# Merging two 256-column matmuls into one of 512 columns in four feed-forward networks, and making the norm's factor on all partitions

## The chip, the cores and the metric

The kernel runs on one core of a Trainium2 chip. Times are device microseconds of one execution, from its start to its end. TensorE (PE in the profile) multiplies matrices, VectorE (DVE), ScalarE (ACT) and GpSimd (POOL) do elementwise work, SyncE (SP) issues the loads of weights.

## What is computed

Two blocks of a network follow one another on a sequence of 256 tokens with 1024 features, in float32. The first block has two layers, each with an FFN, an attention mixer and another FFN; the second block has one mixer and one FFN with a convolution. The part that the change touches is the FFN of the first block, which occurs four times:

```python
def rms_norm(x, g):
    xf = x.astype(jnp.float32)
    y = xf * lax.rsqrt(jnp.mean(xf * xf, axis=-1, keepdims=True) + EPS)
    return (y * g.astype(jnp.float32)).astype(x.dtype)

def swiglu(h, w_gate, w_up, w_down):
    return (jax.nn.silu(h @ w_gate) * (h @ w_up)) @ w_down

    h = rms_norm(x, ffn1_norm[layer])
    x = x + 0.5 * swiglu(h, ffn1_w_gate[layer], ffn1_w_up[layer], ffn1_w_down[layer])
```

The hidden width is 2816, so that gate and up are 1024 x 2816 each and down is 2816 x 1024.

## The kernel before

Features lie on the partitions and the 256 tokens (T) in the columns: `x` is eight tiles of 128 x 256. To keep float32 accuracy with the faster matmul type fp32r, every operand is split in two: a high part (the value rounded to fp32r) and a low part (the rest). A product of two operands then takes three matmuls: high by high, the weights' high part by the activations' low part, the weights' low part by the activations' high part. `mm3` (L301 to L305) issues these three, each with a 128 x 128 block of weights as the stationary operand and 256 columns of activations as the moving one; the program issues a weight load (PEld in the profile) for every matmul.

**Weights.** They arrive as blocks of 128 x 1024 (512 KB), eight stationary blocks each, over five raw buffers (L262). `prep` (L277) makes the high part `wh` on ScalarE (L288) and the low part `wl` mostly on VectorE (L290), in five buffers each; a `wh` can only be written when the matmuls on the block five earlier have ended. A block lasts for eight calls of `mm3`.

**One FFN** (`ffn`, L451). The norm of a row of tokens is one factor per token, so it is applied after the matmul. `norm_tile` (L380) splits `x` times the gain into `xh` (ScalarE, L383) and `xl` (VectorE, L384) and adds up the squares in `acc` on GpSimd (L387, L390). For each of the 22 tiles of 128 hidden features there is a gate product `pg` and an up product `pu`, of eight `mm3` each (`proj_t`, L307). They go round six PSUM banks (`six_ps`): the seventh product of an FFN needs the bank of the first. VectorE multiplies `pg` by the factor `rb` (L464), ScalarE takes the Silu (L466), VectorE multiplies by `pu` (L468), and the result is split into `hh` (ScalarE, L469) and `hl` (VectorE, L470). Then come the eight tiles of the down product, 22 `mm3` each; VectorE scales each (L484), adds it to `x` (L486), and the next norm's split follows. All in all an FFN has 352 + 176 = 528 calls of `mm3`.

**The norm's factor** (`norm_end`, called after the first two products). Two fp32 matmuls with the tokens as stationary columns and a single column of ones (L401) give the sums of squares as a column; ScalarE and GpSimd make the reciprocal root of 128 x 2 numbers (L410 to L416); ScalarE spreads it on a diagonal (L424), and a matmul of ones with that (L430) and a copy (L432) give `rb`, the factor on all partitions.

**Order.** The program is recorded as written above and a scheduler with a model of its own then sets the order on each engine. Every engine executes its own list in order, so an instruction that waits holds up all behind it on that engine. After the last FFN of the first block, `trans_tile` takes the place of `norm_tile`, and the next products (`def_proj`, 258 columns) start on its outputs `dh` and `dl` (L934, L935).

Of the kernel before, what the change touches and what calls it, by code (L numbers as in the profile page):

```python
# [210 lines left out]
class K:  # L211
# [121 lines left out]

    def xh(self, k):
        return self.xht[k // 4][:, (k % 4) * T:(k % 4 + 1) * T]

    def xl(self, k):
        return self.xlt[k // 4][:, (k % 4) * T:(k % 4 + 1) * T]
# [37 lines left out]
    def norm_begin(self):  # L376
        self.xht = [self.slot(f"xh{i}", F32R) for i in range(2)]
        self.xlt = [self.slot(f"xl{i}", F32R) for i in range(2)]
# [65 lines left out]

    def ln_exp_tables(self):

        with self.tc.issue_after(self.last_act.ins):
            self.nc.scalar.preload_act_table_set("natural_log_exp_and_others")


    def ffn(self, next_gain):  # L451
        nc = self.nc
        hh = [self.slot(f"hh{i}", F32R) for i in range(6)]
        hl = [self.slot(f"hl{i}", F32R) for i in range(6)]
        h = lambda t, k: t[k // 4][:, (k % 4) * T:(k % 4 + 1) * T]
        for i in range(KF):
            pg = self.six_ps()[:, :T]
            self.proj_t(pg)
            pu = self.six_ps()[:, :T]
            self.proj_t(pu)  # L460
            if i == 0:
                self.norm_end()
            s = self.tmp("s", T)
            nc.vector.tensor_tensor(out=s, in0=pg, in1=self.rb, op=ALU.mult)  # L464
            sg = self.tmp("sg", T)
            self.last_act = nc.scalar.activation(sg, s, AF.Silu)  # L466
            hp = self.tmp("hp", T)
            nc.vector.tensor_tensor(out=hp, in0=pu, in1=sg, op=ALU.mult)  # L468
            nc.scalar.activation(h(hh, i), hp, AF.Copy)  # L469
            nc.vector.tensor_tensor(out=h(hl, i), in0=hp, in1=h(hh, i).bitcast(F32), op=ALU.subtract)  # L470
# [4 lines left out]
        for j in range(KD):  # L475
            ps = self.mm_ps()[:, :T]
            for k in range(KF):
# [831 lines left out]
    def ffn2(self, first):  # L1309
        nc = self.nc  # L1310
        hh = [self.slot(f"hh{i}", F32R) for i in range(6)]
        hl = [self.slot(f"hl{i}", F32R) for i in range(6)]
        h = lambda t, k: t[k // 4][:, (k % 4) * T:(k % 4 + 1) * T]
        x2 = [self.slot(f"x2n{i}") for i in range(2)]
        for i in range(KF):
# [19 lines left out]
            nc.scalar.activation(h(hh, i), hp, AF.Copy)  # L1335
            nc.vector.tensor_tensor(out=h(hl, i), in0=hp, in1=h(hh, i).bitcast(F32), op=ALU.subtract)
# [13 lines left out]
        for gi, (c0, cw) in enumerate(((0, 512), (512, 256), (768, 256))):  # L1350
            ps = [self.mm_ps()[:, :cw] for _ in range(2)]
            held = []
            for k in range(KF):
# [8 lines left out]
                for tt in range(1 if late else 2):  # L1362
                    self.down(ps[tt], h, hh, hl, k, tt, w)
            for tt in range(2):
                if tt:
                    for k, w in held:
                        self.down(ps[1], h, hh, hl, k, 1, w)
# [28 lines left out]
    def down(self, ps, h, hh, hl, k, tt, w):  # L1396
        s = slice(tt * P, (tt + 1) * P)
        self.mm3n(ps, h(hh, k)[:, s], h(hl, k)[:, s], *w, k == 0, k == KF - 1)
# [84 lines left out]
```

## Time and profile before

| | |
|---|---|
| median of 3 runs | 1401.05 us (1400.18 to 1401.47) |
| the profiled execution | 1400.71 us |
| its span, first to last instruction | 1398.9 us |
| TensorE busy | 1346.7 us, 10278 matmuls |
| VectorE busy | 944.0 us |
| ScalarE busy | 751.7 us |

Some 1.8 us of the profiled execution lie around the span. A row of a timeline gives the start and the length of an instruction in microseconds, the engine, the line, the output and inputs by the program's names, the shape, and in brackets the engine's idle time before it and what ended that. Matmuls are pipelined: a record is longer than the time that the matmul occupies the array, so the pace is read from the distance of two starts, not from the length. "x2" on an fp32 matmul means that it is recorded as two passes. Rows by group give how many instructions there were, their busy time and the mean of one in ns.

### The profile page before, as it was taken

What the parts mean: (1) busy time and instruction counts of PE and PEld (TensorE: products, weight loads), DVE (VectorE), ACT (ScalarE), POOL (GpSimd) and SP (SyncE); (2) the same over time, 40 slices, a digit from 0 to 9 for tenths busy, and PEclk for the clock granted to TensorE, in tenths of its full rate; (3) what the DMA queues carried; (4) which work ended last, traced back from release to release, by engine and by line L of the source; (5) the groups of instructions that cost most, each with busy time, mean ns of one, the idle gap of its engine ahead of it and who ended that gap; (6) DMA issues with size and microseconds to landing.
All of it is one profiled execution on the core that took longest, in us unless ns stands there. A gap on an engine that the chain in (4) does not pass through costs nothing.

```text
span 1398.9 us, 26087 instructions
## 1 busy us (share of the span) xinstructions
PE 1346.7 (96%) x10278; PEld 1283.9 (92%) x10278; DVE 944.0 (67%) x1621; ACT 751.7 (54%) x1300; POOL 304.9 (22%) x371
## 2 busy tenths in 40 slices
PE   6999999699999999999999999999989998989997
PEld 6999998489999999999989899999977888889987
DVE  6666556867666656665549866666778768787754
ACT  5544445655444445444458755445566555666642
POOL 4000045442000110000234340001254114541101
PEclk9999999899999999999999999999999998899999
DMA  7555665125555555655565346655646314265561
GB/s 251 181 182 182 184 192 180 31 76 182 182 182 186 180 186 183 184 181 181 184 228 192 121 151 182 182 184 186 185 154 194 106 47 151 76 183 179 185 213 56
DMA packets 64266, 231.70 MB, mean 166 GB/s; under 512 B 7240, under 2 KB 7376, under 8 KB 64144
## 3 DMA queue, kind: packets, MB, share of 16 engines
q1 hardware_dynamic: 61632, 221.41, 50.6%
q0 software_dynamic: 2512, 8.64, 1.8%
q8 instruction: 80, 1.31, 0.4%
q14 instruction: 42, 0.34, 0.1%
HBM read 228.96 MB, written 1.06 MB: 164 GB/s over the span
## 4 chain that ended last, share of the span: by engine, by line
PE 88%; DVE 6%; POOL 2%; ACT 2%; issue 1%; DMA 0%; DVEq 0%; SPq 0%; ACTq 0%
PE mm L303 19%; PE mm L304 18%; PE mm L305 18%; PE sc L304 5%; PE sc L305 5%; PE sc L303 5%; PE mm L331 4%; PE mm L329 4%; PE mm L330 4%; DVE wl L290 2%; PE mm L557 2%; POOL acc L390 1%; PE aux L548 1%; POOL sq L387 1%; ACT wh L288 1%
## 5 line engine op out<-in xcount | busy, mean ns | idle before, releaser
L288 ACT ACTIVATE wh<-raw 128x1024 fp32r<-128x1024 f32 (+1 forms) x425 | 443.3, 1045 | 512.7 <-issue 255.8
L290 DVE TENSOR_TENSOR wl<-raw,wh 128x1024 fp32r<-128x1024 f32 (+1 forms) x406 | 511.3, 1262 | 272.0 <-ACT wh L288 270.4
L303 PE MATMUL mm<-xh,wh 128*128 128x256 f32 x1328 | 380.0, 287 | 11.2 <-ACT xh L383 5.8
L304 PE MATMUL mm<-xl,wh 128*128 128x256 f32 x1328 | 380.6, 287 | 5.7 <-DVE xl L384 5.5
L305 PE MATMUL mm<-xh,wl 128*128 128x256 f32 x1328 | 378.6, 285 | 0.3 <-DVE wl L290 0.3
L303 PEld LDWEIGHTS mm<-xh,wh 128*128 128x128 f32 x1328 | 257.2, 194 | 14.1 <-issue 6.2
L304 PEld LDWEIGHTS mm<-xl,wh 128*128 128x128 f32 x1328 | 257.2, 194 | 9.2 <-DVE xl L384 7.6
L305 PEld LDWEIGHTS mm<-xh,wl 128*128 128x128 f32 x1328 | 257.5, 194 | 1.4 <-issue 0.7
L303 PE MATMUL mm<-hh,wh 128*128 128x256 f32 x704 | 199.2, 283 | 0.0
L304 PE MATMUL mm<-hl,wh 128*128 128x256 f32 x704 | 199.2, 283 | 0.0
L305 PE MATMUL mm<-hh,wl 128*128 128x256 f32 x704 | 199.2, 283 | 0.0
L303 PE MATMUL sc<-xh,wh 128*128 128x256 f32 x560 | 158.9, 284 | 1.9 <-DVE wgb L955 1.9
L304 PE MATMUL sc<-xl,wh 128*128 128x256 f32 x560 | 159.5, 285 | 0.0
L305 PE MATMUL sc<-xh,wl 128*128 128x256 f32 x560 | 159.2, 284 | 0.0
L387 POOL TENSOR_TENSOR sq<-xt 128x256 f32<-128x256 f32 x48 | 36.5, 763 | 507.3 <-DVE xt L486 472.1
L303 PEld LDWEIGHTS mm<-hh,wh 128*128 128x128 f32 x704 | 135.2, 192 | 0.0
L304 PEld LDWEIGHTS mm<-hl,wh 128*128 128x128 f32 x704 | 135.2, 192 | 0.0
L305 PEld LDWEIGHTS mm<-hh,wl 128*128 128x128 f32 x704 | 135.2, 192 | 0.0
L303 PEld LDWEIGHTS sc<-xh,wh 128*128 128x128 f32 x560 | 107.9, 193 | 2.1 <-ACT xt L911 2.1
L305 PEld LDWEIGHTS sc<-xh,wl 128*128 128x128 f32 x560 | 108.0, 193 | 0.1
L304 PEld LDWEIGHTS sc<-xl,wh 128*128 128x128 f32 x560 | 108.0, 193 | 0.1
L331 PE MATMUL mm<-wh,xl 128*128 128x512 f32 x144 | 56.0, 396 | 2.6 <-DVE xl L913 2.6
(348 smaller groups left out, 2242.7 us busy)
## 6 DMA issues: line engine op xcount, KB each, us to landing
raw<-wst SPq DMA_DIRECT2D x417, 512.0 KB, 3.6
m1b<-m1bias POOLq DMA_DIRECT2D x8, 512.0 KB, 5.2
xt<-xT SPq DMA_DIRECT2D x4, 256.0 KB, 4.9
patf<-m2pat POOLq DMA_DIRECT2D x2, 512.0 KB, 6.9
kb<-scr POOLq DMA_DIRECT2D x2, 512.0 KB, 4.7
out<-x2n SPq DMA_DIRECT2D x4, 256.0 KB, 2.0
raw<-wst SPq DMA_DIRECT2D x2, 256.0 KB, 3.7
m0tab<-m0tab POOLq DMA_DIRECT2D x1, 512.0 KB, 3.9
```

Source lines behind the costliest of these rows:

```text
L288: self.nc.scalar.activation(wh[:, c], r[:, c], AF.Copy)
L290: e.tensor_tensor(out=wl[:, c], in0=r[:, c], in1=wh[:, c].bitcast(F32), op=ALU.subtract)
L303: mm(ps, wh, xh, start=first, stop=False)
L304: mm(ps, wh, xl, start=False, stop=False)
L305: mm(ps, wl, xh, start=False, stop=last)
L329: mm(ps, xh, wh, start=first, stop=False)
L330: mm(ps, xh, wl, start=False, stop=False)
L331: mm(ps, xl, wh, start=False, stop=last)
L387: nc.gpsimd.tensor_tensor(out=sq, in0=self.x(j), in1=self.x(j), op=ALU.mult)
L390: self.last_acc = nc.gpsimd.tensor_tensor(out=acc, in0=sq, in1=self.acc, op=ALU.add)
L548: nc.tensor.transpose(ps[:, kt, qt * P:(qt + 1) * P], p[:, qt, kt * P:(kt + 1) * P], self.ident)
L557: self.nc.tensor.matmul(po[half * 64:half * 64 + 64, :T], v[kt], pT[:, kt], start=kt == 0, stop=kt == 1)
```

## The change

`mm3` is replaced by `mm2` in the gate, up and down products of the four FFNs. The high and low parts of the activations now lie side by side, so that one matmul of the weights' high part takes both as 512 moving columns; its output is a whole PSUM bank whose left half holds the products with the high part and whose right half those with the low part. The weights' low part is still multiplied by the high activations alone, with 256 columns, into the left half. `fold` adds the two halves: ScalarE copies the right half out of PSUM, VectorE adds the left half to it. This is one more instruction on each of the two engines for every product. `norm_bcast` replaces `norm_end` in these four FFNs: one fp32 matmul of a 128 x 128 block of ones with `acc` gives the sum on all partitions, and ScalarE and VectorE make the factor there on 128 x 256. The other stages keep `mm3` and `norm_end`; in the last FFN only the layout of the hidden tiles changes.

```diff
+    def mm2(self, ps, wh, wl, x2, first, last):
+
+        mm = self.nc.tensor.matmul
+        if first:
+            mm(ps, wh, x2, start=True, stop=False)
+        mm(ps[:, :T], wl, x2[:, :T], start=False, stop=False, skip_group_check=True)
+        if not first:
+            mm(ps, wh, x2, start=False, stop=last)
...
-            self.mm3(ps, wh[:, s], wl[:, s], self.xh(k), self.xl(k), k == 0, k == KD - 1)
+            if ps.shape[1] == 2 * T:
+                self.mm2(ps, wh[:, s], wl[:, s], self.x2(k), k == 0, k == KD - 1)
+            else:
+                self.mm3(ps, wh[:, s], wl[:, s], self.xh(k), self.xl(k), k == 0, k == KD - 1)
...
+    def both(t, k):
+        return t[k // 2][:, (k % 2) * 2 * T:(k % 2 + 1) * 2 * T]
...
+    def norm_bcast(self):
+
+        nc = self.nc
+        ps = self.aux_ps()[:, :T]
+        nc.tensor.matmul(ps, self.ones, self.acc, start=True, stop=True)
+        u, y, t = [self.tmp(f"nb{i}", T) for i in range(3)]
+        nc.scalar.activation(u, ps, AF.Identity, scale=1.0 / D, bias=self.eps[:, 0:1])
+        nc.scalar.activation(y, u, AF.Ln)
+        nc.scalar.activation(y, y, AF.Exp, scale=-0.5)
+        nc.vector.scalar_tensor_tensor(out=t, in0=y, scalar=-0.5, in1=y, op0=ALU.mult, op1=ALU.mult)
+        nc.vector.tensor_tensor(out=t, in0=t, in1=u, op=ALU.mult)
+        self.rb = self.tmp("rb", T)
+        nc.vector.scalar_tensor_tensor(out=self.rb, in0=t, scalar=1.5, in1=y, op0=ALU.add, op1=ALU.mult)
...
         for i in range(KF):
-            pg = self.six_ps()[:, :T]
+            pg = self.six_ps()
             self.proj_t(pg)
-            pu = self.six_ps()[:, :T]
+            pu = self.six_ps()
             self.proj_t(pu)
             if i == 0:
-                self.norm_end()
+                self.norm_bcast()
             s = self.tmp("s", T)
-            nc.vector.tensor_tensor(out=s, in0=pg, in1=self.rb, op=ALU.mult)
+            self.fold(s, pg)
+            nc.vector.tensor_tensor(out=s, in0=s, in1=self.rb, op=ALU.mult)
             sg = self.tmp("sg", T)
             self.last_act = nc.scalar.activation(sg, s, AF.Silu)
             hp = self.tmp("hp", T)
-            nc.vector.tensor_tensor(out=hp, in0=pu, in1=sg, op=ALU.mult)
...
+            self.fold(hp, pu)
+            nc.vector.tensor_tensor(out=hp, in0=hp, in1=sg, op=ALU.mult)
...
-                self.mm3(ps, wh[:, s], wl[:, s], h(hh, k), h(hl, k), k == 0, k == KF - 1)
+                self.mm2(ps, wh[:, s], wl[:, s], self.both(h2, k), k == 0, k == KF - 1)
             t = self.tmp("t", T)
-            nc.vector.scalar_tensor_tensor(out=t, in0=ps, scalar=0.5, in1=self.rb,
+            self.fold(t, ps)
+            nc.vector.scalar_tensor_tensor(out=t, in0=t, scalar=0.5, in1=self.rb,
                                            op0=ALU.mult, op1=ALU.mult)
...
+    def fold(self, out, ps):
+
+        self.nc.scalar.activation(out, ps[:, T:], AF.Copy)
+        self.nc.vector.tensor_tensor(out=out, in0=ps[:, :T], in1=out, op=ALU.add)
```

The scheduler sets the order anew. On TensorE, the start of the second product of the first FFN (into the bank `mm_245` before, `mm_236` now), which stands for all products of the four FFNs. Before:

```order
L303 MATMUL mm_245<-xh0_108,wh_191 128x256
L304 MATMUL mm_245<-xl0_110,wh_191 128x256
L305 MATMUL mm_245<-xh0_108,wl_192 128x256
L303 MATMUL mm_245<-xh0_108,wh_191 128x256
L304 MATMUL mm_245<-xl0_110,wh_191 128x256
```

Now:

```order
L305 MATMUL mm_236<-xs0_108,wh_190 128x512
L306 MATMUL mm_236<-xs0_108,wl_191 128x256 x2
L308 MATMUL mm_236<-xs0_108,wh_190 128x512
L306 MATMUL mm_236<-xs1_109,wl_191 128x256
L308 MATMUL mm_236<-xs1_109,wh_190 128x512
```

Three matmuls of 256 columns have become one of 512 and one of 256, and the two lengths alternate; nothing else comes between them.

On ScalarE, from the norm's first step in the second FFN (`ffn20`) to the first two banks that are read. Before, `mm_3720` and `mm_3751` are the first two products, read by VectorE alone:

```order
L410 ACTIVATE nw1_3787<-aux_3782,eps_104 128x2
L288 ACTIVATE wh_3812<-raw_3575 128x1024
L411 ACTIVATE nw0_3786<-nw1_3787 128x2
L412 ACTIVATE nw0_3786<-nw0_3786 128x2
L424 ACTIVATE dg_3796<-ident_95,rc_3785 128x128 x2
L288 ACTIVATE wh_3843<-raw_3621 128x1024
L288 ACTIVATE wh_3882<-raw_3667 128x1024
L432 ACTIVATE rb_3801<-aux_3799 128x256
L466 ACT_TABLE_LOAD
L466 ACTIVATE sg_3805<-s_3803 128x256
```

Now, with `mm_3285` and `mm_3308` as the first two products:

```order
L477 ACTIVATE nb0_3333<-aux_3331,eps_104 128x256
L288 ACTIVATE wh_3356<-raw_3141 128x1024
L478 ACTIVATE nb1_3334<-nb0_3333 128x256
L288 ACTIVATE wh_3379<-raw_3187 128x1024
L479 ACTIVATE nb1_3334<-nb1_3334 128x256
L288 ACTIVATE wh_3414<-raw_3233 128x1024
L535 ACTIVATE s_3343<-mm_3285 128x256
L288 ACTIVATE wh_3437<-raw_3290 128x1024
L505 ACT_TABLE_LOAD
L505 ACTIVATE sg_3347<-s_3343 128x256
L535 ACTIVATE hp_3349<-mm_3308 128x256
```

ScalarE now takes part in emptying the banks (L535), and the first two of these copies stand behind the third and the fourth `wh` after the norm's first step, the second one behind the table load and the Silu as well.

On VectorE, the same place. Before:

```order
L290 TENSOR_TENSOR wl_3844<-raw_3621,wh_3843 128x1024
L290 TENSOR_TENSOR wl_3883<-raw_3667,wh_3882 128x1024
L464 TENSOR_TENSOR s_3803<-mm_3720,rb_3801 128x256
L468 TENSOR_TENSOR hp_3807<-mm_3751,sg_3805 128x256
L464 TENSOR_TENSOR s_3873<-sc_3811,rb_3801 128x256
```

Now:

```order
L480 SCALAR_TENSOR_TENSOR nb2_3335<-nb1_3334 128x256
L481 TENSOR_TENSOR nb2_3335<-nb2_3335,nb0_3333 128x256
L483 SCALAR_TENSOR_TENSOR rb_3341<-nb2_3335,nb1_3334 128x256
L290 TENSOR_TENSOR wl_3415<-raw_3233,wh_3414 128x1024
L536 TENSOR_TENSOR s_3343<-mm_3285,s_3343 128x256
L503 TENSOR_TENSOR s_3343<-s_3343,rb_3341 128x256
L290 TENSOR_TENSOR wl_3438<-raw_3290,wh_3437 128x1024
L536 TENSOR_TENSOR hp_3349<-mm_3308,hp_3349 128x256
```

The factor is now finished on VectorE itself, and each of the first two additions that free a bank (L536) stands behind a `wl`.

## Rows read from the trace of the kernel before

**Rows 1.** The page: span, and busy time, share and instructions of two engines.

```profile
span 1398.9 us, 26087 instructions
...
PE 1346.7 (96%) x10278; PEld 1283.9 (92%) x10278; DVE 944.0 (67%) x1621; ACT 751.7 (54%) x1300; POOL 304.9 (22%) x371
```

**Rows 2.** Windows inside the first three FFNs: length; busy us of each engine; PEclk; DMA.

```profile
22.00:207.00 185.00, 185.00 (x1543) 184.95 (x1542) 112.88 (x151) 88.36 (x123) 18.57 (x26) 1.00 0.62 192
317.00:699.00 382.00, 381.76 (x3175) 381.16 (x3174) 238.77 (x316) 182.18 (x254) 33.89 (x44) 1.00 0.59 184
```

**Rows 3.** Timeline of TensorE in the first FFN, matmuls of 256 columns, 33 starts apart.

```profile
99.93 0.28 PE L303 MATMUL sc<-xh,wh 128*128 128x256 f32 x1
...
103.89 0.28 PE L303 MATMUL sc<-xh,wh 128*128 128x256 f32 x1
```

**Rows 4.** Timeline of TensorE in the last FFN, matmuls of 512 columns, 18 starts apart.

```profile
1329.92 0.39 PE L329 MATMUL mm<-wh,hh 128*128 128x512 f32 x1
...
1334.00 0.39 PE L329 MATMUL mm<-wh,hh 128*128 128x512 f32 x1
```

**Rows 5.** Timeline of TensorE where 256 columns are followed by 512.

```profile
207.81 0.28 PE L305 MATMUL mm<-hh,wl 128*128 128x256 f32 x1
207.93 0.40 PE L329 MATMUL mm<-wh,xh 128*128 128x512 f32 x1
208.16 0.40 PE L330 MATMUL mm<-wl,xh 128*128 128x512 f32 x1
```

**Rows 6.** The same where 512 columns are followed by 256.

```profile
1358.25 0.39 PE L331 MATMUL mm<-wh,hl 128*128 128x512 f32 x1
1358.48 0.28 PE L329 MATMUL mm<-wh,hh 128*128 128x256 f32 x1
1358.59 0.28 PE L330 MATMUL mm<-wl,hh 128*128 128x256 f32 x1
```

**Rows 7.** Timeline of TensorE near the program's start, nine starts apart.

```profile
18.59 0.41 PE L303 MATMUL mm<-xh,wh 128*128 128x256 f32 x1
...
20.51 0.41 PE L303 MATMUL mm<-xh,wh 128*128 128x256 f32 x1
```

**Rows 8.** Timeline of TensorE at the sums of squares of the first norm.

```profile
27.07 0.50 PE L401 MATMUL aux<-ones,acc 128*128 128x1 f32 x4
...
27.64 0.28 PE L304 MATMUL mm<-xl,wh 128*128 128x256 f32 x1
```

**Rows 9.** Timeline of TensorE at the spreading of the second FFN's factor.

```profile
331.51 0.59 PE L430 MATMUL aux<-dg,ones 128*128 128x256 f32 x2
...
332.06 0.28 PE L305 MATMUL mm<-xh,wl 128*128 128x256 f32 x1
```

**Rows 10.** VectorE in 330 to 480 by line and shape: busy us, mean ns, idle before.

```profile
L290 DVE TENSOR_TENSOR wl<-raw,wh 128x1024 fp32r<-128x1024 f32 x53 | 65.6, 1238 | 36.9 <-ACT wh L288 36.8
...
L464 DVE TENSOR_TENSOR s<-mm,rb 128x256 f32<-128x256 f32 x15 | 6.3, 423 | 3.6 <-PE mm L305 3.6
```

**Rows 11.** ScalarE in 330 to 480, the same view.

```profile
L288 ACT ACTIVATE wh<-raw 128x1024 fp32r<-128x1024 f32 x53 | 56.2, 1061 | 76.0 <-issue 57.3 <-PE mm L304 17.6 <-PE sc L304 1.2
L466 ACT ACTIVATE sg<-s 128x256 f32<-128x256 f32 x22 | 8.8, 400 | 0.1
...
L466 ACT ACT_TABLE_LOAD x1 | 1.3, 1283 | 0.0
...
L432 ACT ACTIVATE rb<-aux 128x256 f32<-128x256 f32 x1 | 0.4, 367 | 0.0
```

**Rows 12.** Timeline of VectorE at the second FFN's start, while GpSimd sums squares.

```profile
315.10 0.96 DVE L384 SCALAR_TENSOR_TENSOR xl<-xt,cols,xh 128x256 fp32r<-128x256 f32 x1
...
319.50 1.42 DVE L290 TENSOR_TENSOR wl<-raw,wh 128x1024 fp32r<-128x1024 f32 x1
```

**Rows 13.** Timeline of TensorE at the second FFN's norm, with its wait.

```profile
323.90 0.60 PE L401 MATMUL aux<-ones,acc 128*128 128x1 f32 x4 [0.20 <-POOL acc L390]
```

**Rows 14.** Timeline of TensorE where the last tile of the fourth FFN is waited for.

```profile
1015.66 0.39 PE L304 MATMUL mm<-dl,wh 128*128 128x258 f32 x1 [0.98 <-DVE dl L935]
```

More of the change, by code (lines that the diff above doesn't have):

```diff
@@ L331, in mm3n, with hi, lo, x2 @@
         mm(ps, xl, wh, start=False, stop=last)
+    @staticmethod
+    def hi(t, k):
+        return t[k // 2][:, (k % 2) * 2 * T:(k % 2) * 2 * T + T]
+    @staticmethod
+    def lo(t, k):
+        return t[k // 2][:, (k % 2) * 2 * T + T:(k % 2 + 1) * 2 * T]
+    @staticmethod
+    def both(t, k):
+        return t[k // 2][:, (k % 2) * 2 * T:(k % 2 + 1) * 2 * T]
     def xh(self, k):
-        return self.xht[k // 4][:, (k % 4) * T:(k % 4 + 1) * T]
+        return self.hi(self.xs, k)
     def xl(self, k):
-        return self.xlt[k // 4][:, (k % 4) * T:(k % 4 + 1) * T]
+        return self.lo(self.xs, k)
+    def x2(self, k):
+        return self.both(self.xs, k)
     def x(self, k):
@@ L376, in norm_begin @@
     def norm_begin(self):
-        self.xht = [self.slot(f"xh{i}", F32R) for i in range(2)]
-        self.xlt = [self.slot(f"xl{i}", F32R) for i in range(2)]
+        self.xs = [self.slot(f"xs{i}", F32R) for i in range(KD // 2)]
     def norm_tile(self, j, gain):
@@ L452, in ffn @@
         nc = self.nc
-        hh = [self.slot(f"hh{i}", F32R) for i in range(6)]
-        hl = [self.slot(f"hl{i}", F32R) for i in range(6)]
-        h = lambda t, k: t[k // 4][:, (k % 4) * T:(k % 4 + 1) * T]
+        h2 = [self.slot(f"h{i}", F32R) for i in range(KF // 2)]
         for i in range(KF):
-            pg = self.six_ps()[:, :T]
+            pg = self.six_ps()
             self.proj_t(pg)
-            pu = self.six_ps()[:, :T]
+            pu = self.six_ps()
             self.proj_t(pu)
             if i == 0:
-                self.norm_end()
+                self.norm_bcast()
             s = self.tmp("s", T)
-            nc.vector.tensor_tensor(out=s, in0=pg, in1=self.rb, op=ALU.mult)
+            self.fold(s, pg)
+            nc.vector.tensor_tensor(out=s, in0=s, in1=self.rb, op=ALU.mult)
             sg = self.tmp("sg", T)
@@ L475, in ffn @@
         for j in range(KD):
-            ps = self.mm_ps()[:, :T]
+            ps = self.mm_ps()
             for k in range(KF):
@@ L1310, in ffn2 @@
         nc = self.nc
-        hh = [self.slot(f"hh{i}", F32R) for i in range(6)]
-        hl = [self.slot(f"hl{i}", F32R) for i in range(6)]
-        h = lambda t, k: t[k // 4][:, (k % 4) * T:(k % 4 + 1) * T]
+        h2 = [self.slot(f"h{i}", F32R) for i in range(KF // 2)]
         x2 = [self.slot(f"x2n{i}") for i in range(2)]
@@ L1334, in ffn2 @@
             nc.gpsimd.tensor_tensor(out=hp, in0=y[0], in1=y[1], op=ALU.mult)
-            nc.scalar.activation(h(hh, i), hp, AF.Copy)
-            nc.vector.tensor_tensor(out=h(hl, i), in0=hp, in1=h(hh, i).bitcast(F32), op=ALU.subtract)
+            nc.scalar.activation(self.hi(h2, i), hp, AF.Copy)
+            nc.vector.tensor_tensor(out=self.lo(h2, i), in0=hp, in1=self.hi(h2, i).bitcast(F32), op=ALU.subtract)
             if 8 <= i < 16:
@@ L1362, in ffn2 @@
                 for tt in range(1 if late else 2):
-                    self.down(ps[tt], h, hh, hl, k, tt, w)
+                    self.down(ps[tt], h2, k, tt, w)
             for tt in range(2):
@@ L1366, in ffn2 @@
                     for k, w in held:
-                        self.down(ps[1], h, hh, hl, k, 1, w)
+                        self.down(ps[1], h2, k, 1, w)
                 x = x2[tt][:, c0:c0 + cw]
@@ L1394, in ffn2_out, with down @@
                 nc.sync.dma_start(out=self.aps["out"][0, tt * P:(tt + 1) * P, c], in_=x2[:, c])
-    def down(self, ps, h, hh, hl, k, tt, w):
+    def down(self, ps, h2, k, tt, w):
         s = slice(tt * P, (tt + 1) * P)
-        self.mm3n(ps, h(hh, k)[:, s], h(hl, k)[:, s], *w, k == 0, k == KF - 1)
+        self.mm3n(ps, self.hi(h2, k)[:, s], self.lo(h2, k)[:, s], *w, k == 0, k == KF - 1)
     def proj_t_steps(self, ps):
```

4 lines of the change are left out of this document (2 added, 2 removed).

## The prediction

> **What bounds the kernel now.** I read the page's busy times first: TensorE is busy for 1346.7 of 1398.9 us, the next engine, VectorE, for 944.0 [rows 1]. An average over stages can mislead, so the windows inside the FFNs come next: 185.00 of 185.00 us in the first FFN and 381.76 of 382.00 in the second and third, with the granted clock at 1.00, while VectorE works 61 to 63% of the time and ScalarE 48% [rows 2]. In the FFNs TensorE alone sets the end, and what is asked is the price of one of its instructions. That is in the distance of two starts, since records of neighbours overlap. 33 starts of 256 columns take 103.89 - 99.93 = 3.96 us, 120.0 ns each [rows 3]; 18 starts of 512 columns take 4.08 us, 226.7 ns each [rows 4]. At the granted 1.00 (2.4 GHz) the columns alone would take 106.7 and 213.3 ns, so both lengths pay the same 13.3 ns on top: a price for the instruction, not for its columns. At the program's start 9 starts of 256 columns take 1.92 us, 213.3 ns each [rows 7]. That is the pace of 256 columns at 1.2 GHz, the lower level, without that price (the page's row for the granted clock does not show the level there). The gain is to be had only at the higher pace.
>
> **The change part by part. The products.** Three matmuls of 256 columns, 3 x 120.0 = 360.0 ns, become one of 512 and one of 256, 226.7 + 120.0 = 346.7 ns, with the same 768 columns. That the lengths alternate should cost nothing: a 512 behind a 256 lasts 208.16 - 207.93 = 0.23 us [rows 5], a 256 behind a 512 lasts 1358.59 - 1358.48 = 0.11 us [rows 6]. The saving is 13.3 ns for each of 4 x 528 = 2112 calls. About 14 calls run at the lower pace at the start, those of the first product and of part of the second, with which [rows 7] begin, and gain nothing: 2098 x 13.3 = **27.9 us**, all on the path.
>
> **The fold** adds a ScalarE copy out of PSUM, near the 367 ns of the copy of rb [rows 11], and a VectorE addition, near 423 ns [rows 10], to each of 52 products of an FFN. Per pair of gate and up products TensorE needs 16 x 346.7 = 5.55 us (5.76 before). VectorE then has two wl and five small operations, 2 x 1.24 + 5 x 0.42 = 4.6 us; ScalarE two wh, two small ones and two copies, 2 x 1.06 + 2 x 0.40 + 2 x 0.37 = 3.7 us. Both stay under 5.55, so in the middle of an FFN I cost the fold at nothing: TensorE's own work hides it, with six banks and five buffers of wh between them. If that cover went, each us per pair would cost 88 us.
>
> **The fold at the start of an FFN** is not hidden so well. The seventh product needs the bank of the first, and no bank is emptied until the norm's factor is there. Counting TensorE's work from its last matmul of the mixer in the second FFN's new order, the fifth product ends at 14.3, the sixth at 17.1, the seventh would end at 19.8 us (2.77 us each, and 0.43 for the norm's matmul). ScalarE's list has the third wh behind the norm's first step, which waits for the buffer of the fifth block until 14.3 and ends at 15.4, then the first fold copy (15.75); VectorE makes the wl until 16.65 and the addition until 17.1: in time by nothing. The next wh waits for the sixth block until 17.1 and ends at 18.15; table load 1.28, Silu 0.40 and the second copy 0.37 [rows 11] bring 20.2, the addition 20.6; TensorE wants that bank at 19.8. So it waits **0.8 us**; after that the lists need some 2.3 us per product and catch up. The fourth FFN has the same order, another 0.8. In the third FFN, where a wl stands ahead of the factor's last step, the first bank is 0.4 late and the second 0.3 more: 0.7. In the first FFN the buffers are free earlier and I count nothing. Sum 2.3 us; the bounds are 0 and one whole product, 2.77 us, in each of the four, 11 us.
>
> **The norm.** Before, the two column sums delay TensorE by 0.57 - 0.12 = 0.45 us [rows 8], and the spreading by 0.55 - 0.12 = 0.43 [rows 9]. Now there is one fp32 matmul of the spreading's shape, 0.43. That is 0.45 less in each FFN, **1.8 us**. The waits for acc are 0.20 us at the second FFN, and as much at the fourth [rows 13]; the new order has the matmul 0.9 us of work later there, so they go or stay at 0.4 in all, which I leave out. The chain to the factor itself gets shorter (no GpSimd, no diagonal), but no term hangs on that, since the wh waits above end later.
>
> **Last tiles.** Behind the last down product the copy and the addition lie ahead of the scaling: 0.37 + 0.42 us more before the next stage has its last tile. Ahead of the mixers and of the third FFN, TensorE has two to eight us of other products to do first. At the transition to the second block it has not: it waits already, 0.98 us [rows 14]. There I take **0.8 us** more, between 0 (VectorE's new list has no wl between this addition and dl, where one of 1.2 us stands now) and 2.
>
> **Sum** against the profiled execution, 1400.71 us with its span of 1398.9: -27.9 - 1.8 + 2.3 + 0.8 = -26.6 us, 1374.1. The median of the runs is 0.34 us higher, so I forecast **1374.4 us**.
>
> **The rivals.** *A, hardly anything saved.* The 13.3 ns might belong not to the instruction but to what surrounds it here (the exchange of the stationary block, or reading operands), and come back when two lengths alternate. Speaking for it: no row shows alternation for longer than one step. Against it: both steps have their plain prices [rows 5, 6], and two lengths the same 13.3 [rows 3, 4]. If only a fifth came through, the gain would be 5.6 us less 1.3 of the small terms, 1396.8. The Trainium skill, in "TensorE: Matmul & The Clock Gate", section "Back-to-back issue gap", gives an isolated warm matmul as its columns over 2.4 GHz plus 2.5 ns; by it a call would save 2.5 ns and all calls 5.3 us, this rival's time. The trace differs with 13.3 ns [rows 3, 4], and I go by the trace. That the change does not do what it says is excluded by the new order, which has two matmuls per call.
>
> *B, the banks come late at every FFN*, by a whole product each: 11 us in place of 2.3, 1383. For it: ScalarE is now needed to empty a bank and stands in line behind wh's that wait for TensorE; against it: the margins that I worked out miss by under 1 us.
>
> *C, slower: VectorE becomes the bound.* While GpSimd works beside it at the start of the second FFN, VectorE's wl takes 1.42 us and a small operation up to 0.96 [rows 12]. At such prices a pair would need 2 x 1.42 + 5 x 0.96 = 7.6 us. The break-even is where a pair lasts about 5.76 + 0.13 = 5.9 us, the other gains (704 calls of down products, 9.4 us, and the norms) being spread over 88 pairs. At 6.2 us a pair the time would be 1401 + 88 x 0.3 = 1427. Against it: GpSimd is busy for 34 of 382 us [rows 2], almost all of it outside the gate and up products, and there the plain prices hold [rows 10].
>
> **How the numbers follow.** The forecast with its small terms either way 0.83, A 0.05, B 0.07, C 0.05. With no waits, no loss at the transition and the waits for acc gone the time is 1401.05 - 27.9 - 1.8 - 0.4 = 1370.9; a start that profits a little could add 1. Upwards the range reaches most of the way to B. The range is 1369.5 to 1382, leaving out A, C and the upper half of B, some 0.15. A measurement of this kernel tells about 0.2%, 2.8 us, from no change. Faster by more than that: the forecast, B and most of A, 0.93; the same: a part of A and of C, 0.02; slower: 0.05.
>
> **What would show it.** Right: in the FFNs pairs of starts 346.7 ns apart, with 226.7 and 120.0 alternating; some 8150 matmuls; TensorE idle for some 2 us in all behind VectorE's additions in L536, within 25 us of an FFN's start; VectorE's idle time in the gate and up products short but still there. Wrong: pairs of 355 ns or more (A); waits of 2 us or more on L536 at each FFN (B); TensorE idle all through the gate and up products, with VectorE at 90% or more (C).

## The result, and the profile after

The changed kernel takes 1379.07 us (median of four runs, 1377.88 to 1380.82), the kernel before 1401.0; the ratio is 0.9849, with a 95% interval of 0.9838 to 0.9861. The forecast was 1374.4, in a range of 1369.5 to 1382. So it is faster, as forecast, by 22.0 us where 26.6 had been worked out, and the time lies inside the range. The sum behind it was less good than that sounds: two terms were too favourable by some 11 us together, and a gain of 6 us that no step had foreseen took their place. Without that gain the time would have been some 1385 us, above the range; that it lies inside is luck.

The profiled execution after is the slowest of the four, 1380.82 us, span 1379.0; against the profiled one of before, 1400.71, that is 19.9 us. All that follows is measured between these two. The page's busy times, answering to [rows 1], and the windows inside the first three FFNs, answering to [rows 2] (the columns are the same):

```profile
PE 1327.5 (96%) x8150; PEld 1166.1 (85%) x8150; DVE 1012.8 (73%) x1841; ACT 807.6 (59%) x1496; POOL 308.1 (22%) x355
```

```profile
22.00:200.00 178.00, 177.28 (x1010) 153.94 (x1009) 129.63 (x205) 101.11 (x170) 15.16 (x14) 1.00 0.58 193
316.00:685.00 369.00, 367.56 (x2092) 319.18 (x2092) 270.82 (x419) 208.69 (x348) 36.74 (x34) 1.00 0.56 187
```

There are 8150 matmuls where some 8150 were expected; TensorE is busy for all but 0.7 of 178 and 1.4 of 369 us, and VectorE for 73%. The bound is the same as before. Where the 19.9 us came from is told by the starts of marker matmuls in the two traces (first and last matmul of each down product, last one of each mixer's output product):

| stretch | before, us | after, us | difference | by the prediction's terms |
|---|---|---|---|---|
| start, gate and up of the first FFN | 144.57 | 141.83 | -2.7 | |
| gate and up of the second, third, fourth | 128.45, 127.71, 128.45 | 124.89, 124.93, 124.88 | -3.6, -2.8, -3.6 | all four: -18.5 - 1.8 + 2.3 |
| down, four times | 63.24 each | 61.75, three times, 61.54 | -6.2 | -9.4 |
| the two mixers of the first block | 107.87, 121.73 | 108.50, 121.80 | +0.7 | 0 |
| transition and mixer of the second block | 162.56 | 167.24 | +4.7 | +0.8 |
| its norm and the last FFN's gate and up | 154.23 | 147.82 | -6.4 | 0 |
| last down products, end | 70.40 | 70.39 | 0 | 0 |

**The pace.** Timeline of TensorE, the first matmuls (L305) of five gate and up products, then of two down products:

```profile
60.71 0.39 PE L305 MATMUL mm<-xs,wh 128*128 128x512 f32 x1
...
105.45 0.39 PE L305 MATMUL mm<-xs,wh 128*128 128x512 f32 x1
...
108.27 0.40 PE L305 MATMUL mm<-xs,wh 128*128 128x512 f32 x1
...
111.05 0.39 PE L305 MATMUL mm<-xs,wh 128*128 128x512 f32 x1
...
157.21 0.39 PE L305 MATMUL mm<-h,wh 128*128 128x512 f32 x1
...
164.98 0.39 PE L305 MATMUL mm<-h,wh 128*128 128x512 f32 x1
```

From 60.71 to 111.05 there are 18 products of eight calls, 349.6 ns per call, where 346.7 had been worked out. The loss is not spread evenly: one product takes 2.82 us (353 ns per call), the next 2.78 (347), and so on in turns. In the down products 22 calls take 7.77 us, 353 ns per call, in all tiles but the first one to three of each FFN, which run near 347. So a call is at one of two paces, and only the faster one is what the prediction had.

**The waits for the banks** by line and releaser, in us in total, count and longest:

```profile
PE mm L305 <- DVE hp L536: 2.2, 3, 0.7
...
PE sc L305 <- DVE s L536: 0.3, 1, 0.3
...
PE sc L305 <- DVE hp L536: 0.3, 1, 0.3
```

They make 2.8 us, where 2.3 had been forecast: 0.7 in each of the four FFNs.

**The transition**, answering to [rows 14]: TensorE's waits, then ScalarE's and VectorE's work on the last down tile, whose last matmul starts at 993.60, then windows of 10 us of the changed kernel (columns as in rows 2; the column behind the five engines is the granted clock):

```profile
998.60 0.38 PE L312 MATMUL mm<-dh,wh 128*128 128x258 f32 x1 [2.08 <-ACT dh L980]
999.42 0.39 PE L313 MATMUL mm<-dl,wh 128*128 128x258 f32 x1 [0.44 <-DVE dl L981]
```

```profile
994.03 1.06 ACT L288 ACTIVATE wh<-raw 128x1024 fp32r<-128x1024 f32 x1 [1.38 <-PE mm L308]
995.00 0.36 ACT L535 ACTIVATE t<-mm 128x256 f32<-128x256 f32 x1
...
995.12 1.23 DVE L290 TENSOR_TENSOR wl<-raw,wh 128x1024 fp32r<-128x1024 f32 x1 [1.47 <-ACT wh L288]
996.27 0.42 DVE L536 TENSOR_TENSOR t<-mm,t 128x256 f32<-128x256 f32 x1
```

```profile
993.00:1003.00 10.00, 7.47 (x50) 6.93 (x49) 5.79 (x10) 4.43 (x8) 2.11 (x5) 0.90 0.35 119
1003.00:1013.00 10.00, 10.00 (x62) 9.52 (x62) 3.81 (x7) 4.00 (x8) 1.94 (x7) 0.76 0.33 109
```

The fold's copy (L535) stands behind a `wh` and its addition (L536) behind a `wl`, which had itself waited for that `wh`. TensorE waits 2.52 us in place of 0.98. And then its granted clock falls: 0.90 and 0.76 over 20 us, which means that for a part of them it ran at 1.2 GHz. At 2.4 GHz the same work would have taken 1.0 + 2.4 = 3.4 us less. Before, the two windows from 1011 to 1031 show 1.00. Wait and clock together, 1.5 + 3.4 us, are near the 4.7 us of that stretch; the agreement is not exact, since a later wait of TensorE in it (for `xl` before, `xs` now) went from 2.58 to 1.60 us.

**The second block's FFN**, which the change does not touch beyond the layout of its activations. Before: ScalarE, VectorE, and TensorE's wait.

```profile
1220.74 1.06 ACT L288 ACTIVATE wh<-raw 128x1024 fp32r<-128x1024 f32 x1 [2.43 <-PE mm L304]
1221.71 0.59 ACT L1326 ACTIVATE s<-dv,cols 128x256 f32<-128x256 f32 x1
```

```profile
1227.07 5.05 DVE L290 TENSOR_TENSOR wl<-raw,wh 128x1024 fp32r<-128x1024 f32 x2
1232.04 0.47 DVE L1327 SCALAR_TENSOR_TENSOR s<-mm,cols,s 128x255 f32<-128x255 f32 x1
...
1233.44 0.56 PE L303 MATMUL mm<-xh,wh 128*128 128x256 f32 x1 [4.45 <-DVE s L1329]
```

After, the same two engines:

```profile
1204.57 0.59 ACT L1370 ACTIVATE s<-dv,cols 128x256 f32<-128x256 f32 x1
...
1205.56 1.05 ACT L288 ACTIVATE wh<-raw 128x1024 fp32r<-128x1024 f32 x1
```

```profile
1209.99 2.06 DVE L290 TENSOR_TENSOR wl<-raw,wh 128x1024 fp32r<-128x1024 f32 x1 [1.30 <-ACT wh L288]
1211.98 0.47 DVE L1371 SCALAR_TENSOR_TENSOR s<-mm,cols,s 128x255 f32<-128x255 f32 x1
```

Before, ScalarE sat for 2.43 us in front of a `wh` that waited for TensorE, with the third pair of convolution copies (`s<-dv`) behind it, and VectorE did two `wl`, 2.5 us each while GpSimd worked on weight blocks too, ahead of the first convolution that empties a PSUM bank. After, the copies stand ahead of the `wh`, one `wl` and not two stands directly ahead of that convolution, and the idle time of 4.45 us is gone. With it went a loss of clock: windows of 10 us, the first before, from just ahead of the end of that idle time, the second of the changed kernel at the same work.

```profile
1233.00:1243.00 10.00, 9.56 (x68) 9.59 (x69) 7.87 (x16) 6.18 (x13) 3.35 (x3) 0.83 0.64 208
1213.00:1223.00 10.00, 10.00 (x86) 10.00 (x85) 10.00 (x15) 7.14 (x14) 5.65 (x3) 1.00 0.73 238
```

A granted clock of 0.83 over 10 us is 1.7 us lost. Idle time and clock, 4.45 + 1.7 us, make up nearly all of the 6.4. Was that the change's doing?

### The profile page after: what moved, and what is told of

It is laid out like the page before. It is cut to its first block, busy times and chain, and to the rows that moved or that the text cites. A ratio compares the mean times of both kernels' runs of the same rounds, so it can differ in the third digit from the quotient of the medians.

```text
span 1379.0 us, 22443 instructions
## 1 busy us (share of the span) xinstructions
PE 1327.5 (96%) x8150; PEld 1166.1 (85%) x8150; DVE 1012.8 (73%) x1841; ACT 807.6 (59%) x1496; POOL 308.1 (22%) x355
## 4 chain that ended last, share of the span: by engine, by line
PE 90%; DVE 6%; ACT 2%; issue 1%; DMA 0%; POOL 0%; DVEq 0%; SPq 0%; ACTq 0%
PE mm L308 25%; PE mm L306 14%; PE sc L308 7%; PE mm L312 5%; PE mm L313 5%; PE mm L314 5%; PE sc L306 4%; PE mm L343 4%; PE mm L341 4%; PE mm L342 4%; PE mm L305 3%; PE mm L603 2%; DVE wl L290 1%; PE sc L313 1%; PE sc L314 1%
## 5 line engine op out<-in xcount | busy, mean ns | idle before, releaser
L308 PE MATMUL mm<-xs,wh 128*128 128x512 f32 x826 | 297.7, 400 | 3.2 <-DVE xs L410 3.2
L306 PE MATMUL mm<-xs,wl 128*128 128x256 f32 x944 | 245.5, 281 | 0.0
L308 PE MATMUL mm<-h,wh 128*128 128x512 f32 x672 | 237.9, 398 | 0.0
L306 PE MATMUL mm<-h,wl 128*128 128x256 f32 x704 | 191.5, 280 | 0.0
L306 PEld LDWEIGHTS mm<-xs,wl 128*128 128x128 f32 x944 | 179.7, 190 | 10.6
L308 PEld LDWEIGHTS mm<-xs,wh 128*128 128x128 f32 x826 | 155.8, 189 | 36.9 <-DVE xs L410 5.4
L308 PEld LDWEIGHTS mm<-h,wh 128*128 128x128 f32 x672 | 126.0, 188 | 29.2
L308 PE MATMUL sc<-xs,wh 128*128 128x512 f32 x406 | 144.8, 396 | 0.0
L306 PEld LDWEIGHTS mm<-h,wl 128*128 128x128 f32 x704 | 132.9, 189 | 3.1
L312 PE MATMUL mm<-xs,wh 128*128 128x256 f32 x384 | 110.5, 289 | 1.0 <-ACT wh L288 0.8
L313 PE MATMUL mm<-xs,wh 128*128 128x256 f32 x384 | 110.2, 287 | 0.1
L314 PE MATMUL mm<-xs,wl 128*128 128x256 f32 x384 | 109.6, 286 | 0.3 <-DVE wl L290 0.3
L312 PEld LDWEIGHTS mm<-xs,wh 128*128 128x128 f32 x384 | 73.8, 193 | 3.6 <-issue 1.5
L313 PEld LDWEIGHTS mm<-xs,wh 128*128 128x128 f32 x384 | 74.0, 193 | 1.6 <-issue 0.8
L314 PEld LDWEIGHTS mm<-xs,wl 128*128 128x128 f32 x384 | 74.0, 193 | 1.3 <-issue 0.7
```

What stands on the lines that cost most here:

```text
L306: mm(ps[:, :T], wl, x2[:, :T], start=False, stop=False, skip_group_check=True)
L308: mm(ps, wh, x2, start=False, stop=last)
```

## The experiments

The kernels stand in the order in which they answer the questions: the pace, the norm, the transition, the second block's FFN, and a better version. Medians are given with those of before in the same session, 1400.3 to 1400.8 us.

**One order for all calls** (`e1_same_order`). The changed kernel issues a product as 512, 256, then 256, 512 for each further call: the lengths alternate except for a doubled 512 and a doubled 256 at each product's start. Here they alternate without a break.

```diff
-        if first:
-            mm(ps, wh, x2, start=True, stop=False)
-        mm(ps[:, :T], wl, x2[:, :T], start=False, stop=False, skip_group_check=True)
-        if not first:
-            mm(ps, wh, x2, start=False, stop=last)
+        mm(ps, wh, x2, start=first, stop=last)
+        mm(ps[:, :T], wl, x2[:, :T], start=False, stop=last, skip_group_check=True)
```

> Every call now issues 512 columns, then 256, the first of a product too, so that the lengths alternate without a break from one product to the next. Theory 1 (the doubled 512 and the doubled 256 at the start of each product switch the matmuls between two phases, one with 346.7 and one with 353.4 ns for a pair): all products of a stage have the same spacing, either 346.7 (some 2112 x 3.5 = 7 us less than the changed kernel, 1372) or 353.4 (some 4 to 5 us more, 1383 to 1384). Theory 2 (each change of length costs some ns, wherever it stands): the mean stays near 350 to 351 ns and the time within 1 us of the changed kernel, 1379. Theory 3 (the PSUM bank or the buffer of the weights sets the price): gate and up products still take turns between 346.7 and 353.4.

Measured: 1386.74 us (1381.91 to 1391.36), ratio to before 0.9902 (0.9870 to 0.9933). Timeline of TensorE, two 256-column matmuls 80 calls apart:

```profile
99.99 0.28 PE L305 MATMUL sc<-xs,wl 128*128 128x256 f32 x1
...
128.26 0.28 PE L305 MATMUL mm<-xs,wl 128*128 128x256 f32 x1
```

28.27 us for 80 calls are 353.4 ns each, and all gate and up products but the first few of an FFN run so. No products take turns any more, but the pace is not the slower one for all: the down products of the second, third and fourth FFN run at 346.6 ns per call from their second tile on, those of the first FFN at 353. Theory 1 holds; banks and weight buffers rotate as before and no longer matter, so theory 3 falls. Most of the added time does not come from the pace. The profiled execution is the slowest of four that lie 9.5 us apart; in it the third FFN's gate and up stretch takes 4.1 us more than in the changed kernel, with a wait of 2.7 us for a bank (L533, the fold's addition there), and the second block's norm, gate and up 3.6 us more, with a wait of 2.64 us (`dg`) that the changed kernel does not have, since the scheduler ordered the other engines anew.

**Grouped by length** (`e2_grouped`): the first 512, then the eight 256 of a block of weights, then the other 512.

```diff
+        for k, wh, wl, x2 in calls:
+            if k == 0:
+                mm(ps, wh, x2, start=True, stop=False)
+        for k, wh, wl, x2 in calls:
+            mm(ps[:, :T], wl, x2[:, :T], start=False, stop=False, skip_group_check=True)
+        for k, wh, wl, x2 in calls:
+            if k:
+                mm(ps, wh, x2, start=False, stop=k == n - 1)
```

> Within a block of weights all 256-column matmuls stand together and then all 512-column ones; only two changes of length are left in a gate or up product in place of thirteen. Theories 1 and 2 (what is lost comes with the alternation): 226.7 and 120.0 ns within the groups, 8 calls in 2.773 us or a few ns more, so that the time falls by some 2112 x 3.5 = 7 us to 1372. Theory 3 (the bank or the buffer sets the price): every second product keeps some 53 ns extra, time near 1379.

Measured: 1388.49 us (1388.38 to 1391.31), ratio 0.9919 (0.9905 to 0.9934). Timeline of one product and the start of the next; a row with x8 or x7 is a run of that many matmuls:

```profile
85.56 0.39 PE L305 MATMUL mm<-xs,wh 128*128 128x512 f32 x1
85.79 1.12 PE L307 MATMUL mm<-xs,wl 128*128 128x256 f32 x8
86.74 1.78 PE L310 MATMUL mm<-xs,wh 128*128 128x512 f32 x7
88.35 0.39 PE L305 MATMUL mm<-xs,wh 128*128 128x512 f32 x1
```

Eight 256 take 0.95 us, 119 ns each as before; seven 512 take 1.61 us, 230 ns each and not 226.7. In the single starts the first five 512 behind a run of 256 are 233, 236, 228, 233 and 231 ns apart, and only the sixth and seventh 227. So a change of length is paid over several matmuls behind it, 20 ns per product in all, 349 ns per call. No single step showed that [rows 5, 6]. The expected 7 us did not come. And the time is 9 us above the changed kernel, mainly because TensorE again waits 4.4 us in the second block's FFN, and 2.8 us for a bank in the third FFN; with the lower clock behind these waits the two stretches are 8.1 and 3.3 us longer.

**Several orders in one kernel** (`e7_orders`). The swap makes 512, 512, 256, 256 out of two calls of a strictly alternating product, once in each of the first three FFNs; the fourth has "pair" (512, 256, 256, 512) and "quad" (two 512, four 256, two 512).

```diff
+        if pat == "pair":
+            o = []
+            for a in range(0, n, 2):
+                q = ks[a:a + 2]
+                o += [("h", q[0])] + [("l", k) for k in q] + [("h", k) for k in q[1:]]
+            return o
+        o = [(c, k) for k in ks for c in "hl"]
+        if pat.startswith("flip"):
+            a = 2 * int(pat[4:])
+            o[a + 1], o[a + 2] = o[a + 2], o[a + 1]
+        return o
```

> Several orders of the same matmuls in one kernel, each FFN with its own, read as ns per call (one 512 and one 256). First three FFNs: strict alternation, with one swap (512, 512, 256, 256) in the thirteenth gate or up product, at its first, second or third pair of calls. Fourth FFN: 512, 256, 256, 512 in pairs of calls for 22 products and four down tiles, then groups of four. Theory 1 (two stable rhythms, 346.7 and 353.4, and a break in the alternation can move TensorE from one to the other): strict alternation holds 353.4 up to the swap, and behind the swap at least one of the three FFNs stays at 346.7 until the next irregular place. Theory 2 (a change of length costs some ns each time): a swap changes nothing behind itself; pairs give half the loss of alternation (about 350), fours a quarter (348.4).

Measured: 1380.65 us in the one run. Starts in the first FFN behind the swap; in the second from ahead of the swap to the swap's doubled 512, then behind it; in the third behind it; in the fourth with pairs and with groups of four:

```profile
60.12 0.28 PE L329 MATMUL mm<-xs,wl 128*128 128x256 f32 x1
...
115.59 0.28 PE L329 MATMUL sc<-xs,wl 128*128 128x256 f32 x1
...
336.43 0.39 PE L327 MATMUL sc<-xs,wh 128*128 128x512 f32 x1
...
347.87 0.62 PE L327 MATMUL mm<-xs,wh 128*128 128x512 f32 x2
...
370.00 0.28 PE L329 MATMUL mm<-xs,wl 128*128 128x256 f32 x1
...
436.08 0.28 PE L329 MATMUL mm<-xs,wl 128*128 128x256 f32 x1
...
542.08 0.28 PE L329 MATMUL sc<-xs,wl 128*128 128x256 f32 x1
...
625.28 0.28 PE L329 MATMUL sc<-xs,wl 128*128 128x256 f32 x1
...
829.25 0.63 PE L327 MATMUL mm<-xs,wh 128*128 128x512 f32 x2
...
868.26 0.63 PE L327 MATMUL mm<-xs,wh 128*128 128x512 f32 x2
...
876.65 0.63 PE L329 MATMUL sc<-xs,wl 128*128 128x256 f32 x4
...
932.78 0.63 PE L329 MATMUL mm<-xs,wl 128*128 128x256 f32 x4
```

With the same strict alternation behind the swap the first FFN runs at 55.47 us for 160 calls, 346.7 ns, the second at 66.08 for 187, 353.4, the third at 83.20 for 240, 346.7. Ahead of their swaps the first and the third ran at 353; the second ran at 346.7, 33 calls in 11.44 us up to the doubled 512 at 347.87. So each of the three swaps turned the pace round, two to the faster and one to the slower, and there it stayed to the end of the gate and up products. A short wait can do the same: the second had come to 346.7 behind a wait of 0.64 us for a bank at 333.58, ahead of which it ran at 353. So theory 1 is shown: TensorE has two lasting rhythms for the same sequence, and a break in the sequence moves it from one to the other. The changed kernel has such a break at each product's start, which is why its products take turns. Pairs take 39.01 us for 112 calls, 348.3 ns, fours 56.13 for 160, 350.8. Theory 2 wanted it the other way round.

**The norm alone** (`e3_norm_alone`): the kernel before with `norm_bcast` in its FFNs.

```diff
-                self.norm_end()
+                self.norm_bcast()
```

> The kernel before with the norm's new factor alone; products as before, three matmuls of 256 columns per call. By the prediction's sum 0.45 us less in each of four FFNs, 1.8 us, 1399.3. If the order of the other work moves with it, the idle time of 4.5 us that TensorE has before the second block's FFN tells whether that idle time hangs on the chain of the norm (it goes, 1395) or on the products (it stays).

Measured: 1392.35 us (1392.12 to 1392.63), ratio 0.9942 (0.9925 to 0.9958). The gate and up stretches of the second, third and fourth FFN are each 0.43 to 0.45 us shorter, which is the term of the prediction; the first FFN's cannot be told from the scatter of its stretch. The rest of the 8.5 us is elsewhere: 6.2 us in the second block's FFN, which has no idle time of 4.5 us here, and 1.2 us in the stretch from the start to the end of the first FFN's gate and up products, which varies by itself (below).

**The products alone** (`e4_products_alone`): the changed kernel with the old chain to the factor, the same line turned round.

> The changed kernel with the old chain to the factor (column sums, diagonal, spreading). By the prediction's sum 1.8 us more than the changed kernel for the norm's matmuls, 1380.9. The banks of the first two products then wait for a longer chain with GpSimd in it: if the waits for the banks hang on this chain they grow from 2.8 us in all to 5 or more (1383 and up), if on ScalarE's weight blocks they stay near 2.8.

Measured: 1392.91 us (1392.17 to 1393.43), ratio 0.9946 (0.9931 to 0.9961), 13.8 us above the changed kernel, where 1.8 had been expected. Some 8 us of that are the second block's FFN, with its idle time of 4.4 us and a lower clock behind it. The waits for the banks grow to 6.8 us:

```profile
PE mm L305 <- DVE s L536: 4.4, 3, 2.4
...
PE sc L305 <- DVE s L536: 2.4, 1, 2.4
```

With the fold, the first bank hangs on the factor: 2.4 us in the first and the third FFN, 1.0 in the other two. The prediction had said that no term hangs on this chain, and with the new chain none does; but the new chain is what keeps the waits at 2.8.

**The last tile of the fourth FFN without the fold** (`e6_last_tile`), the other 31 tiles as in the changed kernel:

```diff
+                if whole:
                     self.mm2(ps, wh[:, s], wl[:, s], self.both(h2, k), k == 0, k == KF - 1)
+                else:
+                    self.mm3(ps, wh[:, s], wl[:, s], self.hi(h2, k), self.lo(h2, k), k == 0, k == KF - 1)
             t = self.tmp("t", T)
-            self.fold(t, ps)
+            if whole:
+                self.fold(t, ps)
```

> The changed kernel, with the last tile of the fourth FFN's down product done the old way: three matmuls of 256 columns per call, no fold. That costs 22 x 7 ns = 0.15 us. Theory (the 4.7 us lost at the transition and in the mixer after it are the fold's two instructions behind weight blocks, and the lower clock that the longer idle time brings): 3 to 4.5 us less than the changed kernel, 1374.5 to 1376, with the granted clock at 1.00 behind the transition. Rival (the loss is the mixer's new order, or the clock falls for another reason): within 1 us of the changed kernel.

Measured: 1375.34 us (1375.05 to 1375.72), ratio 0.9828 (0.9812 to 0.9844), 3.7 us below the changed kernel. TensorE's wait, and the windows behind it:

```profile
998.04 0.39 PE L313 MATMUL mm<-dl,wh 128*128 128x258 f32 x1 [0.98 <-DVE dl L986]
```

```profile
993.00:1003.00 10.00, 9.02 (x75) 8.81 (x74) 5.78 (x10) 5.21 (x9) 3.04 (x5) 1.00 0.48 165
1003.00:1013.00 10.00, 9.67 (x76) 8.99 (x75) 7.21 (x12) 3.91 (x8) 6.41 (x10) 1.00 0.36 124
```

The wait is the 0.98 us of before [rows 14], the clock stays at 1.00, and the stretch takes 162.27 us, where it took 162.56 before and 167.24 in the changed kernel. The loss was the fold's two instructions in their queues, with the clock that fell behind the longer idle time.

**The kernel before, in another order** (`e5_before_hold`, `e8_before_hold2`). In the first, the weight blocks that the second block's FFN asks for itself stand on ScalarE behind the copies of the six products that are there already; in the second, one `wl` also stands on VectorE behind the first convolution that reads a bank.

```diff
+            with self.tc.issue_after(self.hold.ins) if self.hold else nullcontext():
+                self.nc.scalar.activation(wh[:, c], r[:, c], AF.Copy)
...
+            with self.tc.issue_after(self.hold_v.ins) if b == self.start["ffn2"] + 14 else nullcontext():
+                e.tensor_tensor(out=wl[:, c], in0=r[:, c], in1=wh[:, c].bitcast(F32), op=ALU.subtract)
```

> The kernel before, with one order constraint and nothing else: the weight blocks that the second block's FFN asks for itself (the twelfth and later) stand on ScalarE behind the six convolution copies instead of ahead of the third pair; three or four rows of ScalarE's list and one of VectorE's move. Theory (the changed kernel's gain of 6.4 us in that FFN is this order, not the change): TensorE's idle time of 4.5 us there goes, 4.5 to 6.4 us less than before, 1394.5 to 1396.5. Rival (the idle time comes from the work ahead, which the change has made shorter): it stays, 1401 within 1.

Measured: 1398.09 us (1397.11 to 1400.14), ratio 0.9988 (0.9979 to 0.9998). The wait shrinks to 3.0 us and does not go; two `wl` still stand ahead of the convolution:

```profile
1224.89 5.10 DVE L292 TENSOR_TENSOR wl<-raw,wh 128x1024 fp32r<-128x1024 f32 x2
1229.91 0.47 DVE L1331 SCALAR_TENSOR_TENSOR s<-mm,cols,s 128x255 f32<-128x255 f32 x1
...
1231.31 0.36 PE L305 MATMUL mm<-xh,wh 128*128 128x256 f32 x1 [2.97 <-DVE s L1333]
```

> The kernel before with the constraint of e5_before_hold and a second one of the same kind on VectorE: of the two weight blocks (wl) that stand ahead of the first convolution read from a PSUM bank, the second goes behind it, as it stands in the changed kernel. e5_before_hold left 3.0 us of the idle time, behind two wl that took 5.10 us beside GpSimd. Theory (the whole gain of 6.4 us in the second block's FFN is the order on ScalarE and VectorE): the rest of the idle time goes too, the stage takes 5.5 to 6.5 us less than before, 1394 to 1396. Rival (something else in the change ends it): 3 us of idle time remain, 1398.

Measured: 1394.27 us (1393.39 to 1394.88), ratio 0.9954 (0.9939 to 0.9968). The wait is gone and the stretch takes 146.31 us, 7.9 less than before. Some 1.6 of these are the clock further ahead, 0.74 in place of 0.66 from 1175 to 1195 us, which I put down to no edit; by the medians the whole gain is 6.1 us. So the kernel before can have this gain by two constraints of order, without the change. The other runs agree: in `e2_grouped` and `e4_products_alone` the `wh` stands ahead of the third pair of copies, as before, and the idle time is 4.4 us; in `e3_norm_alone` it stands behind, and there is none.

**A better order** (`e9_pairs_down`, `e10_pairs_all`). Both have `e6_last_tile`'s last tile; the first issues the down products in pairs of calls, the second the gate and up products too.

```diff
+        for a, b in zip(calls[::2], calls[1::2]):
+            mm(ps, a[1], a[3], start=a[0] == 0, stop=False)
+            for k, wh, wl, x2 in (a, b):
+                mm(ps[:, :T], wl, x2[:, :T], start=False, stop=False, skip_group_check=True)
+            mm(ps, b[1], b[3], start=False, stop=b[0] == n - 1)
```

> e6_last_tile, with the down products alone in the order 512, 256, 256, 512; the orders on ScalarE, VectorE and GpSimd stay the same instruction for instruction. By e7_orders this order takes 348.3 ns per call where the down products have 352.8 now: (704 - 22) x 4.5 = 3.1 us less than e6_last_tile, 1372.3. If the rhythm of the down products hangs on something else than the order, no change, 1375.3.

Measured: 1373.93 us (1373.41 to 1374.31), ratio 0.9809 (0.9794 to 0.9823), 1.4 us below `e6_last_tile`, not 3.1. The down products of the four FFNs give 2.3 us (61.10 in place of 61.75 three times, 61.45 in place of 61.80); 3.1 was worked out from 352.8 ns for all tiles, but the first tile of each FFN had run near 347 already. The second block's mixer gave 1.5 us back, its clock at 0.96 in the first 40 us where `e6_last_tile` has 1.00. That mixer took 1.2 us longer in `e5_before_hold` than before, too, in nothing but the same work, with the clock at 0.96 in another part; so this is scatter of that stretch, and I put it down to no edit.

> As e9_pairs_down, and the gate and up products in the order 512, 256, 256, 512 too, 348.3 ns per call where these have 349.65 now: 1408 x 1.35 = 1.9 us less than e9_pairs_down, 1370.4, if the scheduler's order of the rest does not move; it moves a little, and where a bank is waited for by a further weight block at an FFN's start, as in e1_same_order and e2_grouped, some 3 us are lost again.

Measured: 1369.61 us (1369.28 to 1370.11), ratio to before 0.9777 (0.9761 to 0.9794), the fastest of all, 9.5 us below the changed kernel. Two first matmuls of pairs, 92 calls apart:

```profile
100.12 0.40 PE L313 MATMUL sc<-xs,wh 128*128 128x512 f32 x1
...
132.17 0.40 PE L313 MATMUL sc<-xs,wh 128*128 128x512 f32 x1
```

32.05 us for 92 calls are 348.4 ns each. The waits for the banks fell as well, to 1.4 us, and the stretch with the transition and the mixer is 1.4 us shorter than in `e9_pairs_down`.

## Why the prediction was right, and where it was not

**The products: right mechanism, wrong size.** "That the lengths alternate should cost nothing" is the step that failed. It was read off one step from 256 to 512 and one from 512 to 256 [rows 5, 6]. Sustained, a call takes 349.6 ns in gate and up and 353 in most of the down products, in place of 346.7. The term was 27.9 us and measured 20.7: 1394 calls at 360.0 - 349.6 ns, 14.5 us, and 6.2 us in the down products (between the starts of their first and last matmul; the last one is now longer, and with it the gain is some 0.4 us less). That is 9.9 ns per call where the sum had 13.3. `e1_same_order` and `e7_orders` show that the same sequence runs at 353.4 or at 346.7 ns. The changed kernel has a break at each product's start, and its gate and up products take turns between the two; its down products are nearly all slow. This was what rival A put in doubt, at a third of the size that A gave it. The Trainium skill gives an isolated warm matmul 2.5 ns on top of its columns ("TensorE: Matmul & The Clock Gate", section "Back-to-back issue gap"); by that, as an estimate, the products would have saved 5.3 us. The traces disagree: some 20 us.

**The fold in the middle of an FFN: right.** TensorE waits for no bank there, and VectorE, at 73%, still has idle time. Rival C did not come.

**The banks at an FFN's start: right in size.** 2.8 us against 2.3; the first FFN has 0.7, where nothing was counted. Rival B's mechanism is real but conditional: 2.4 to 2.8 us in one or two FFNs as soon as the chain to the factor is the old one (`e4_products_alone`) or another order has the bank wait (`e1_same_order`, `e2_grouped`, `e7_orders`).

**The norm: right.** 0.43 to 0.45 us in each of three FFNs in `e3_norm_alone`, 1.8 in all if the first gives as much. The waits for `acc` are gone from the list, a chance of 0.4 us that was left out.

**The transition: the wait right, its price wrong.** The wait grew by 1.54 us, inside the bounds of 0 to 2. What the term left out is the clock: 3.4 us by the two windows, spent at the lower level behind the longer idle time. The stretch measured 4.7 in place of 0.8, and `e6_last_tile` takes it away whole.

**The second block's FFN: not foreseen.** 6.4 us of the gain, 4.45 of them a wait and 1.7 the clock behind it, were made where the diff changes nothing but a layout. The prediction looked at the order only near the FFNs of the first block. `e8_before_hold2` shows that the order on two engines suffices for this gain.

Against the sum of -26.6 us that is 7.2 for the products, 0.5 for the banks, 3.9 for the transition, 0.7 in the mixers, and -6.4: -20.7, where -19.9 was measured. The remaining 0.8 is near what the start and first FFN alone vary by with nothing changed in them (-0.4 and +0.4 us in `e5_before_hold` and `e8_before_hold2`).

## What to carry to other kernels

The price of an instruction in a uniform run is not its price in a mixed one: before building on it, look for a long run of the very sequence, or try two or three orders of it, which cost nothing but the order. When a scheduler orders a program anew, compare the two traces stretch by stretch before the change is credited with anything; here 6 us of 20 came from a place that it did not touch. A wait of the engine that sets the end is priced with the clock that it may cost behind it.

## What the hardware showed that I had not expected

TensorE keeps one of two paces for the same alternating sequence of 512 and 256 columns, 346.7 or 353.4 ns per call, over at least 240 calls, and a swap of two matmuls (three of three in `e7_orders`) or a short wait (0.64 us there) moved it from one to the other. In the slow rhythm starts repeat every three calls (113, 233, 117, 241, 120, 236 ns), in the fast one every two (117, 231, 112, 233 ns). Behind a run of 256 the first five 512 pay 1 to 9 ns each on top of 226.7. What in the engine holds these rhythms the runs do not tell, and it stays open; of what was tried, neither the PSUM bank nor the weights' buffer decides.

The granted clock of the changed kernel fell to 0.76 in a window of 10 us behind waits of 2.08 and 0.44 us with one matmul between them, and stayed at 1.00 behind one wait of 0.98 us at the same place in `e6_last_tile`. The length of the wait does not decide it alone: `e3_norm_alone` and `e10_pairs_all` have the wait of 0.98 us too, and there the clock fell behind it, for half as much. The window of `e10_pairs_all`, whose wait ends at 991.50:

```profile
987.00:997.00 10.00, 9.02 (x64) 8.81 (x63) 5.08 (x9) 4.47 (x8) 3.03 (x5) 0.83 0.47 157
```

The stretch from the transition to the mixer's end took 165.1 to 168.4 us in the five kernels with the two waits, and 162.3 to 163.8 in the seven with one of 0.98 or 1.00 us. So the price of some 1.5 us more of idle time is not fixed: 4.7 us in the two executions compared, 1.3 to 6.1 over all.
